# Attention in a hybrid backbone block: the weighted values of two query tiles in one product, with the values stationary

## The chip, the cores and the metric

The kernel runs on one core of a Trainium2 chip. A core has TensorE (PE in the profile, with its weight loads as PEld), VectorE (DVE), ScalarE (ACT), GpSimd (POOL), and SyncE (SP), which issues most DMA transfers. The metric is the device time of one launch in microseconds. The times known beforehand are 1080.52, 1079.1 and 1081.81 us: median 1080.52.

## The reference

The block has two layers over 1024 latent tokens of width 1024 and 256 context tokens. The even layer is a Fourier mixer and a differential attention side by side; the odd layer is a gated short convolution. The change concerns the attention alone:

```python
def one_block(qblk):
    s = jnp.einsum('bqhmd,bkhmd->bhmqk', qblk, k,
                   preferred_element_type=jnp.float32) * ATTN_SCALE
    p = jax.nn.softmax(s, axis=-1)
    a = p[:, :, 0] - lam * p[:, :, 1]
    return jnp.einsum('bhqk,bkhv->bqhv', a.astype(v.dtype), v)
...
ao = (rms_norm(attn_o, subln_g) * (1.0 - lam_init)).reshape(b, n, ATT_WIDTH)
y = jnp.concatenate([fo, ao], axis=-1) * jax.nn.silu(proj[..., G0:])
return y @ w_out
```

There are 4 heads. Each has two score maps (m = 0, 1) of 64 features, 1280 keys (256 of the context, 1024 latent), 1024 queries and values of 128 features. The second softmax is subtracted from the first with a learned factor; the weighted values are normalised by their RMS over the 128 features, scaled by a gain per feature, multiplied by a gate, and projected.

## The kernel before

A query tile is 128 queries of one head: 32 tiles, `i` = 0 to 31, eight to a head. Four tiles make a group `g` (half of a head's queries): eight groups. Keys come in ten blocks of 128 (`NK`). The keys and queries of the scores are float32 values split in two and stored in the rounded type fp32r (the profile prints them as f32 too); the weights `p`, their transposes `aT` and the values `v` are plain float32. The profile shows each plain float32 product as two passes, that is two weight loads and two matmuls.

In the attention loop the order of the work on TensorE, VectorE, ScalarE and GpSimd is written out by hand: an engine runs its instructions in the order in which the functions below are called (`manual_schedule(engines=MANUAL)`, L957). For a tile `i`:

- `score(i, m)` (L1025, L1026): twelve fp32r products in all for m = 0 and 1, into the PSUM tile S0 or S1. There is one S tile for each m, so the score of tile i+1 waits until `expo(i, m)` has read it.
- `rowmax(i, m)` (L1030): VectorE takes the negated row maximum over the 1280 keys. `expo(i, m)` (L1041): ScalarE takes the exponential and, by its accumulator, the row sum z.
- `combine(i)` (L1048 to L1055), called in the next tile: p0 minus lambda times z0/z1 times p1. VectorE does the first 1024 keys, GpSimd the last 256. The division by z0 is left to the RMS step, which cancels it but for the epsilon.
- `turn(i, c)` (L1065, L1067): TensorE transposes up to four key blocks of p0 into one PSUM bank (`ps_t`), ScalarE copies them to `aT`. Three turns of 4, 4 and 2 blocks make a tile.
- `values(i)` (L1075, L1084): ten products with the transposed weights stationary and 128 columns of `v` moving, into `ps_av` (queries on partitions); VectorE copies the result to a quarter of `o`.
- `squares(i)` (L1090): ScalarE squares that quarter and sums each row.
- `fin_a(g)` (L1096 to L1101) on GpSimd: the RMS factor from the sums and z0, its power -0.5, and the product with `o`.
- `fin_b(g)` (L1109 to L1115): four transposes of `o` into `ps_o`, product with gain and gate on VectorE, and the split into `yh` and `yl` for the output projection.

`turn`, `values` and `squares` lag the score by two or three tiles. `ps_t`, `ps_av` and `ps_o` all take turns in the two PSUM banks of the pool `pst` under the tag "t"; a new tile waits for the readers of the one that had its bank. The loads of the next head's keys, queries and values go through SP, 13 per head, three per tile from a head's third tile on. Behind the loop (L1186 on) the last tiles' turns and values are woven into the first two products of the output projection (`proj_feat2`, L1128 to L1130); the first of them needs groups 0, 2, 4 and 6 for its last four steps.

The broadcast of a row factor over the partitions by a diagonal (`rms_diag`, `ps_rows`, L228) and sums over partitions by a product with a column of ones (`token_sums`, L209) are used elsewhere in the kernel.

Of the kernel before, what the change touches and what calls it, by code (L numbers as in the profile page):

```python
# [33 lines left out]
S_C, S_G, S_B, S_CW, S_SUB, S_QG, S_KG, S_L = 0, 16, 32, 80, 104, 105, 169, 233  # L34
# [3 lines left out]
def block_kernel(tc, A):  # L38
    nc = tc.nc
# [34 lines left out]
    small = const.tile([P, S_N], F32, name="small")  # L74
# [3 lines left out]
    sel, ident = cst[:, 0:2], cst[:, 2:2 + P]  # L78
# [83 lines left out]
    wq, W, wsrc = [], [], []  # L162
# [857 lines left out]
    def score(i, m):  # L1020
        ks, qs, _ = preps[i // 8]
        q = qs[m][:, (i % 8) * P:(i % 8 + 1) * P]
        for c0, cn in CH:
            kc = slice(c0, c0 + cn)
            nc.tensor.matmul(S[m][:, kc], lhsT=q, rhs=ks[m][0][:, kc], start=True, stop=False)  # L1025
            nc.tensor.matmul(S[m][:, kc], lhsT=q, rhs=ks[m][1][:, kc], start=False, stop=True)  # L1026

    def rowmax(i, m):
        nm = av.tile([P, 1], F32, name=f"nm{m}", bufs=2)
        nc.vector.tensor_reduce(out=nm, in_=S[m][:, :NKEY], op=ALU.max, axis=AX.X, negate=True)  # L1030
        tiles[i, m, "nm"] = nm

    def expo(i, m):
        p = (pp, av)[m].tile([P, NKEY], F32, name=f"p{m}", bufs=(4, 2)[m])
        if m == 0:
            if i % 4 == 0:
                z0s[i // 4] = av.tile([P, 4], F32, name="z0", bufs=3)
            z = z0s[i // 4][:, i % 4:i % 4 + 1]
        else:
            z = av.tile([P, 1], F32, name="z1", bufs=2)  # L1040
        nc.scalar.activation(out=p, in_=S[m][:, :NKEY], func=AF.Exp, bias=tiles.pop((i, m, "nm")), accum_out=z)  # L1041
        tiles[i, m] = (p, z)
# [12 lines left out]
        nc.vector.scalar_tensor_tensor(out=p0[:, ks], in0=p1[:, ks], scalar=c, in1=p0[:, ks], op0=ALU.mult,  # L1055
                                       op1=ALU.add)

    def turn(i, c):

        n = min(4, NK - 4 * c)  # L1060
        pt = pst.tile([P, NB], F32, name="ps_t", tag="t", bufs=2)
        p0 = tiles[i, 0][0]
        for j in range(n):
            k = 4 * c + j
            nc.tensor.transpose(pt[:, j * P:(j + 1) * P], p0[:, k * P:(k + 1) * P], ident)  # L1065
        at = av.tile([P, NB], F32, name="aT", bufs=4)
        nc.scalar.copy(out=at[:, :n * P], in_=pt[:, :n * P])  # L1067
        groups[i, c] = at

    def values(i):  # L1070
        g, j = divmod(i, 4)
        v = preps[i // 8][2]
        ps = pst.tile([P, NB], F32, name="ps_av", tag="t", bufs=2)[:, :P]
        for k in range(NK):
            nc.tensor.matmul(ps, lhsT=groups[i, k // 4][:, (k % 4) * P:(k % 4 + 1) * P],  # L1075
                             rhs=v[:, k * P:(k + 1) * P], start=k == 0, stop=k == NK - 1)
# [7 lines left out]
        nc.vector.tensor_copy(out=o[:, j, :], in_=ps)  # L1084

    def squares(i):
        g, j = divmod(i, 4)
        o, ss, _ = groups[g, "f"]
        sq = av.tile([P, P], F32, name="osq", bufs=1)
        nc.scalar.activation(out=sq, in_=o[:, j, :], func=AF.Square, accum_out=ss[:, j:j + 1])  # L1090

    def fin_a(g, eng=nc.gpsimd):

        o, ss, _ = groups[g, "f"]
        z0 = z0s.pop(g)
        nc.gpsimd.tensor_tensor(out=z0, in0=z0, in1=z0, op=ALU.mult)  # L1096
        nc.gpsimd.tensor_scalar(out=z0, in0=z0, scalar1=EPS, scalar2=None, op0=ALU.mult)
        nc.gpsimd.tensor_scalar(out=ss, in0=ss, scalar1=1.0 / DV, scalar2=None, op0=ALU.mult)
        nc.gpsimd.tensor_tensor(out=ss, in0=ss, in1=z0, op=ALU.add)
        nc.gpsimd.tensor_tensor(out=ss, in0=ss, in1=mhalf[:, 0:4], op=ALU.pow)  # L1100
        eng.tensor_tensor(out=o, in0=o, in1=ss.unsqueeze(2).broadcast_to([P, 4, P]), op=ALU.mult)  # L1101

    def fin_b(g):

        f, half = NH + g // 2, g % 2
        o, _, sg = groups.pop((g, "f"))
        pt = pst.tile([P, NB], F32, name="ps_o", tag="t", bufs=2)
        for j in range(4):
            nc.tensor.transpose(pt[:, j * P:(j + 1) * P], o[:, j, :], ident)  # L1109
        y = av.tile([P, NB], F32, name="y", bufs=1)  # L1110
        nc.vector.scalar_tensor_tensor(out=y, in0=pt, scalar=g08, in1=sg, op0=ALU.mult, op1=ALU.mult)
        yh = yao.tile([P, NB], F32R, name="yh", tag="y", bufs=16)
        nc.scalar.copy(out=yh, in_=y)
# [43 lines left out]
    for i in range(NQ):  # L1157
        if i % 8 == 0 and i // 8 + 1 < NH:
            loads = att_prep(i // 8 + 1, nc.sync)
        if i % 8 > 1:  # L1160
            for _ in range(min(3, len(loads))):
                loads.pop(0)()
        score(i, 0)
        if i >= 2:
            turn(i - 2, 0)
            turn(i - 2, 1)
        rowmax(i, 0)
        if i:
            combine(i - 1)
        if i >= 3:  # L1170
            squares(i - 3)
        if i >= 6 and i % 4 == 2:
            fin_a((i - 6) // 4)
# [6 lines left out]
        if i >= 2:  # L1180
            values(i - 2)
        if i >= 7 and i % 4 == 3:
            fin_b((i - 7) // 4)
# [14 lines left out]
    pend = [proj_feat2(W[0], 0, {1: lambda: turn(NQ - 2, 2), 2: lambda: values(NQ - 2), 4: lambda: turn(NQ - 1, 0),
                                 5: lambda: (turn(NQ - 1, 1), squares(NQ - 2)), 7: lambda: turn(NQ - 1, 2)})]
    values(NQ - 1)  # L1200
    squares(NQ - 1)
# [560 lines left out]
```

## Time and profile before

| | before |
|---|---|
| median of three runs | 1080.52 us |
| the profiled execution, its span | 1081.25 us, 1079.4 us |
| TensorE, weight loads | 1031.8 us (96%), 843.3 us |
| VectorE, ScalarE, GpSimd | 760.0, 480.7, 436.8 us |
| value products (L1075), 640 passes | 76.8 us of modelled length |
| transposes of the weights (L1065), in the loop's 29 tiles | 290, 41.2 us of modelled length |
| first score of tile 2 to first score of tile 31 | 378.68 to 551.54 us |

The span is shorter than the time of the execution by what lies before the first and behind the last instruction. Busy shares are averages over stages with different limits. Lengths of matmuls overlap one another in the records, so what a matmul costs in a full stream is read from the distance between starts. A group's row gives the line, engine, operation, tiles, shapes and count, then the busy time, the mean length in ns, and the idle time ahead of it with what ended it.

### The profile page before, as it was taken

Reading aid. Unit: us, or ns where it says so; the run is one execution under the profiler, and the core shown is the slowest. Engines: PE = TensorE matmul, PEld = TensorE weight load, DVE = VectorE, ACT = ScalarE, POOL = GpSimd, SP = SyncE. Lnnn points to the kernel's source line nnn. Section 1 sums busy time; section 2 is a strip of 40 time slices with the busy share of each in tenths; the row PEclk is TensorE's granted clock in tenths of the full one; section 3 lists DMA queues with packets and bytes.
Section 4 is the critical chain, followed back from the end, with each engine's and each line's share of the span. In section 5 each row is a group of like instructions: output and inputs, shape, how many; then the busy total and the mean of one; then the engine's idle time right before and its main releaser. Section 6 shows DMA issues by size and latency. Waiting matters only on the chain.

```text
span 1079.4 us, 14123 instructions
## 1 busy us (share of the span) xinstructions
PE 1031.8 (96%) x5128; PEld 843.3 (78%) x5128; DVE 760.0 (70%) x1112; ACT 480.7 (45%) x876; POOL 436.8 (40%) x379
## 2 busy tenths in 40 slices
PE   6989999989999899999999999999999999998898
PEld 3667888878887699899988878777888888786676
DVE  4599956957888288888873386996555554579953
ACT  4453234312445377777763363634333333343420
POOL 1257115530454047775666644034443543402031
PEclk9999999999999999999999999999999999998999
DMA  9823896354111987081004643021112111113421
GB/s 335 339 97 117 253 370 225 108 152 136 43 61 66 249 196 177 25 190 52 18 21 156 198 156 134 0 78 60 59 39 75 43 60 59 59 39 107 145 99 58
DMA packets 61380, 131.12 MB, mean 121 GB/s; under 512 B 5248, under 2 KB 30208, under 8 KB 58112
## 3 DMA queue, kind: packets, MB, share of 16 engines
q1 hardware_dynamic: 60240, 125.64, 36.7%
q0 software_dynamic: 1072, 4.59, 1.2%
q8 instruction: 40, 0.66, 0.3%
q14 instruction: 28, 0.23, 0.1%
HBM read 105.57 MB, written 24.64 MB: 121 GB/s over the span
## 4 chain that ended last, share of the span: by engine, by line
PE 64%; DVE 21%; POOL 4%; ACT 4%; issue 3%; DMA 3%; SPq 0%; ACTq 0%; POOLq 0%; DVEq 0%
PE psX L657 6%; PE psX L659 6%; PE psX L658 6%; PE ps_av L1075 5%; PE ps_tok L284 3%; PE ps_tok L285 3%; PE ps_tok L286 3%; PE psY L658 3%; PE psY L659 3%; PE psY L657 3%; PE S L1025 3%; PE S L1026 3%; DVE nm L1030 2%; PE ps_t L1065 2%; DMA ada_raw<-in_ada_dram 2%
## 5 line engine op out<-in xcount | busy, mean ns | idle before, releaser
L284 PE MATMUL ps_tok<-whi,hhi 128*128 128x512 f32 x288 | 118.0, 410 | 2.5 <-ACT hhi L393 1.5
L285 PE MATMUL ps_tok<-whi,hlo 128*128 128x512 f32 x288 | 115.0, 399 | 3.5 <-DVE hlo L397 3.5
L286 PE MATMUL ps_tok<-wlo,hhi 128*128 128x512 f32 x288 | 114.8, 399 | 0.6 <-DVE wlo L172 0.4
L634 POOL TENSOR_TENSOR s<-wraw 128x512 f32<-128x512 f32 x20 | 26.7, 1333 | 212.5 <-DMA wraw<-in_wodd_dram 101.7
L1030 DVE TENSOR_REDUCE nm<-S 128x1 f32<-128x1280 f32 x64 | 95.2, 1487 | 22.0 <-PE S L1026 17.2
L1041 ACT ACTIVATE p<-S,nm 128x1280 f32<-128x1280 f32 x64 | 85.1, 1330 | 44.7 <-DVE nm L1030 40.9
L61 ACT CAST wop<-wraw 128x512 fp32r<-128x512 f32 x106 | 65.2, 619 | 82.7 <-PE ps_feat L1130 22.0
L657 PE MATMUL psX<-B,wop 128*128 128x512 f32 x240 | 95.6, 398 | 5.0 <-ACT u L1366 2.5
L659 PE MATMUL psX<-B,wop 128*128 128x512 f32 x240 | 95.3, 397 | 4.3 <-DVE wop L1312 4.3
L658 PE MATMUL psX<-B,wop 128*128 128x512 f32 x240 | 94.8, 395 | 0.0
L62 POOL TENSOR_TENSOR wop<-wraw,wop 128x512 fp32r<-128x512 f32 x52 | 71.5, 1377 | 42.1 <-ACT wop L61 42.0
L1075 PE MATMUL ps_av<-v,aT 128*128 128x128 f32 x640 | 76.8, 276 | 0.0
L1075 PEld LDWEIGHTS ps_av<-v,aT 128*128 128x128 f32 x640 | 74.2, 192 | 0.2
L285 PEld LDWEIGHTS ps_tok<-whi,hlo 128*128 128x128 f32 x288 | 55.1, 191 | 16.8 <-DVE hlo L397 6.0
L284 PEld LDWEIGHTS ps_tok<-whi,hhi 128*128 128x128 f32 x288 | 55.3, 192 | 16.2 <-issue 2.2
L1052 POOL TENSOR_TENSOR p<-p,cc 128x256 f32<-128x256 f32 x32 | 40.3, 1259 | 64.7 <-DVE cc L1049 45.1
L286 PEld LDWEIGHTS ps_tok<-wlo,hhi 128*128 128x128 f32 x288 | 55.1, 191 | 13.1 <-DVE wlo L172 1.4
L658 PE MATMUL psY<-B,wop 128*128 128x512 f32 x160 | 63.6, 397 | 1.7 <-DVE B L1259 1.7
L659 PE MATMUL psY<-B,wop 128*128 128x512 f32 x160 | 63.5, 397 | 0.0
L657 PE MATMUL psY<-B,wop 128*128 128x512 f32 x160 | 63.5, 397 | 0.0
L657 PEld LDWEIGHTS psX<-B,wop 128*128 128x128 f32 x240 | 45.1, 188 | 18.3 <-ACT u L1366 3.4
L659 PEld LDWEIGHTS psX<-B,wop 128*128 128x128 f32 x240 | 45.0, 188 | 17.0 <-DVE wop L1312 6.2
(354 smaller groups left out, 2694.5 us busy)
## 6 DMA issues: line engine op xcount, KB each, us to landing
ada_raw<-in_ada_dram SPq DMA_DIRECT2D x24, 1024.0 KB, 7.6
wraw<-in_wodd_dram SPq DMA_DIRECT2D x32, 512.0 KB, 3.5
wraw<-in_wo_dram SPq DMA_DIRECT2D x24, 512.0 KB, 4.1
wraw<-in_wtok_dram SPq DMA_DIRECT2D x16, 512.0 KB, 5.3
arena<-kd SPq DMA_DIRECT2D x16, 320.0 KB, 9.0
kq<-kd SPq DMA_DIRECT2D x16, 320.0 KB, 10.2
xt<-in_xT_dram SPq DMA_DIRECT2D x16, 256.0 KB, 6.3
xr<-in_xT_dram SPq DMA_DIRECT2D x16, 256.0 KB, 4.0
```

Of the source, the lines that this page charges most:

```text
L61: nc.scalar.copy(out=o[:, 0, :], in_=src)
L62: eng.tensor_tensor(out=o[:, 1, :], in0=src, in1=f32(o[:, 0, :]), op=ALU.subtract)
L284: nc.tensor.matmul(ps, lhsT=hh, rhs=whi, start=k == 0, stop=False)
L285: nc.tensor.matmul(ps, lhsT=hl, rhs=whi, start=False, stop=False)
L286: nc.tensor.matmul(ps, lhsT=hh, rhs=wlo, start=False, stop=k == KT - 1)
L657: nc.tensor.matmul(ps, lhsT=a, rhs=x[k][0], start=start and k == 0, stop=False, skip_group_check=not start)
L658: nc.tensor.matmul(ps, lhsT=a, rhs=x[k][1], start=False, stop=False, skip_group_check=not start)
L659: nc.tensor.matmul(ps, lhsT=b, rhs=x[k][0], start=False, stop=k == 3, skip_group_check=not start)
L1030: nc.vector.tensor_reduce(out=nm, in_=S[m][:, :NKEY], op=ALU.max, axis=AX.X, negate=True)
L1041: nc.scalar.activation(out=p, in_=S[m][:, :NKEY], func=AF.Exp, bias=tiles.pop((i, m, "nm")), accum_out=z)
L1052: nc.gpsimd.tensor_tensor(out=p1[:, ks], in0=p1[:, ks], in1=c.broadcast_to([P, POOLK]), op=ALU.mult)
L1075: nc.tensor.matmul(ps, lhsT=groups[i, k // 4][:, (k % 4) * P:(k % 4 + 1) * P], rhs=v[:, k * P:(k + 1) * P], start=k == 0, stop=k == NK - 1)
```

## The change

Query tiles are handled in pairs (`a` even, tiles a and a+1). A turn now transposes two key blocks of both tiles into one bank, so there are five turns of four transposes per pair, all copied as 128x512. `values` takes a block of `v` as the stationary operand and 256 columns of `aT` as the moving one, so `ps_av` comes out with the value features on partitions and the queries of two tiles along the row. `outputs` scales by the gain (per partition) on VectorE and squares on ScalarE, both straight from PSUM. The sum of squares over the features is now a sum over partitions: `fin_m` does four products with the squares stationary and one column of ones moving. `fin_d` adds the epsilon term, takes the power, and builds four diagonals on GpSimd; `fin_r` multiplies an all-ones matrix with them, which spreads the factor over the partitions; `fin_b` multiplies and splits as before. No output transposes are left. The gate is multiplied into `o` by `fin_a`. The factor 1/128 of the mean moves into the gain and the epsilon.

In an odd tile i (a = i-3) the loop does turns 0 to 3 of a pair and one of `fin_m` and `fin_r`; in the next, even tile it does turn 4 and all twenty passes of the pair's values, eight ahead of score(i,1) and twelve behind it. `outputs` follows in the next odd tile. `fin_b` stands ahead of `expo(i, 1)` on ScalarE. The new PSUM tile `ps_m` has the tag "t" too. `aT` has five buffers in place of four.

```diff
+    def turn(a, c):
         pt = pst.tile([P, NB], F32, name="ps_t", tag="t", bufs=2)
+        for n in range(4):
+            k, p0 = 2 * c + n // 2, tiles[a + n % 2, 0][0]
+            nc.tensor.transpose(pt[:, n * P:(n + 1) * P], p0[:, k * P:(k + 1) * P], ident)
+        at = av.tile([P, NB], F32, name="aT", bufs=5)
+        nc.scalar.copy(out=at, in_=pt)
+        groups[a, c] = at
+    def values(a, keys):
+        v = preps[a // 8][2]
+        if keys[0] == 0:
+            groups[a, "ps"] = pst.tile([P, NB], F32, name="ps_av", tag="t", bufs=2)[:, :2 * P]
+        for k in keys:
+            nc.tensor.matmul(groups[a, "ps"], lhsT=v[:, k * P:(k + 1) * P],
+                             rhs=groups[a, k // 2][:, (k % 2) * 2 * P:(k % 2 + 1) * 2 * P], start=k == 0,
+                             stop=k == NK - 1)
+    def outputs(a):
...
+        nc.vector.tensor_scalar(out=o[:, qs], in0=ps, scalar1=g08, scalar2=None, op0=ALU.mult)
+        nc.scalar.activation(out=sq[:, qs], in_=ps, func=AF.Square)
+    def fin_z(g):
+        z0 = z0s[g]
+        nc.gpsimd.tensor_tensor(out=z0, in0=z0, in1=z0, op=ALU.mult)
+        nc.gpsimd.tensor_scalar(out=z0, in0=z0, scalar1=EPS * DV, scalar2=None, op0=ALU.mult)
     def fin_a(g, eng=nc.gpsimd):
+        o, _, sg = groups[g, "f"]
+        eng.tensor_tensor(out=o, in0=o, in1=sg, op=ALU.mult)
+    def fin_m(g):
+        ps, sq, z0 = pst.tile([P, NB], F32, name="ps_m", tag="t", bufs=2)[:, :4], groups[g, "f"][1], z0s.pop(g)
+        for j in range(4):
+            nc.tensor.matmul(ps[:, j:j + 1], lhsT=sq[:, j * P:(j + 1) * P], rhs=ones[:, 0:1], start=True, stop=True)
+        groups[g, "m"] = ps, z0
+    def fin_d(g):
+        ps, z0 = groups.pop((g, "m"))
+        nc.vector.tensor_tensor(out=z0, in0=ps, in1=z0, op=ALU.add)
+        nc.gpsimd.tensor_tensor(out=z0, in0=z0, in1=mhalf[:, 0:4], op=ALU.pow)
+        dg = groups[g, "d"] = av.tile([P, 4, P], F32, name="dg", bufs=1)
+        nc.gpsimd.tensor_tensor(out=dg, in0=ident.unsqueeze(1).broadcast_to([P, 4, P]),
+                                in1=z0.unsqueeze(2).broadcast_to([P, 4, P]), op=ALU.mult)
+    def fin_r(g):
+        ps = groups[g, "r"] = pst.tile([P, NB], F32, name="ps_o", tag="t", bufs=2)
+        nc.tensor.matmul(ps, lhsT=ones, rhs=groups.pop((g, "d")).rearrange("p j d -> p (j d)"), start=True, stop=True)
     def fin_b(g):
+        y, _, _ = groups.pop((g, "f"))
+        nc.vector.tensor_tensor(out=y, in0=groups.pop((g, "r")), in1=y, op=ALU.mult)
         yh = yao.tile([P, NB], F32R, name="yh", tag="y", bufs=16)
         nc.scalar.copy(out=yh, in_=y)
...
+        odd, a = i % 2, i - 3 - (i + 1) % 2
         score(i, 0)
+        if a >= 2 and odd:
+            outputs(a - 2)
+        if a >= 0 and odd:
+            turn(a, 0)
+            turn(a, 1)
+        elif a >= 0:
+            turn(a, 4)
+            values(a, range(0, 4))
         rowmax(i, 0)
         if i:
             combine(i - 1)
+        if a >= 4 and a % 4 == 0 and odd:
+            fin_a((a - 4) // 4)
+        if a >= 2 and a % 4 == 2 and not odd:
+            fin_z((a - 2) // 4)
         expo(i, 0)
         score(i, 1)
+        if a >= 0 and odd:
+            turn(a, 2)
+            turn(a, 3)
+            if a >= 4 and a % 4 == 0:
+                fin_m((a - 4) // 4)
+            elif a >= 6:
+                fin_r((a - 6) // 4)
+        elif a >= 0:
+            values(a, range(4, NK))
         rowmax(i, 1)
+        if a >= 4 and a % 4 == 0 and odd:
+            fin_d((a - 4) // 4)
+        if a >= 6 and a % 4 == 2 and odd:
+            fin_b((a - 6) // 4)
         expo(i, 1)
...
+    turn(NQ - 4, 4)
+    values(NQ - 4, range(NK))
+    fin_r(NG - 2)
+    fin_b(NG - 2)
+    outputs(NQ - 4)
     combine(NQ - 1)
+    fin_z(NG - 1)
...
+    pend = [proj_feat2(W[0], 0, {2: lambda: turn(NQ - 2, 0), 3: lambda: turn(NQ - 2, 1),
+                                 4: lambda: turn(NQ - 2, 2), 5: lambda: turn(NQ - 2, 3),
+                                 6: lambda: turn(NQ - 2, 4)})]
+    values(NQ - 2, range(NK))
+    outputs(NQ - 2)
     fin_a(NG - 1, nc.vector)
+    pend.append(proj_feat2(W[1], 0, {2: lambda: (fin_m(NG - 1), fin_d(NG - 1)), 7: lambda: fin_r(NG - 1)}))
```

More of the change, by code (lines that the diff above doesn't have):

```diff
@@ L264, in lam @@
         nc.vector.tensor_scalar(out=neglam, in0=neglam, scalar1=-LAM0, scalar2=None, op0=ALU.add)
-        nc.vector.tensor_scalar(out=g08, in0=small[:, S_SUB:S_SUB + 1], scalar1=1.0 - LAM0, scalar2=None,
+        nc.vector.tensor_scalar(out=g08, in0=small[:, S_SUB:S_SUB + 1], scalar1=(1.0 - LAM0) * DV ** 0.5, scalar2=None,
                                 op0=ALU.mult)
@@ L1056, in combine @@
                                        op1=ALU.add)
-    def turn(i, c):
-        n = min(4, NK - 4 * c)
+    def turn(a, c):
         pt = pst.tile([P, NB], F32, name="ps_t", tag="t", bufs=2)
[L1062 to L1076, printed above, removed]
+        for n in range(4):
+            k, p0 = 2 * c + n // 2, tiles[a + n % 2, 0][0]
+            nc.tensor.transpose(pt[:, n * P:(n + 1) * P], p0[:, k * P:(k + 1) * P], ident)
@@ L1077, in values @@
+    def outputs(a):
+        g, j = divmod(a, 4)
         if j == 0:
-            o = av.tile([P, 4, P], F32, name="o", bufs=2)
-            ss = av.tile([P, 4], F32, name="ss", bufs=2)
+            o = av.tile([P, NB], F32, name="o", bufs=2)
+            sq = av.tile([P, NB], F32, name="osq", bufs=1)
             sg = av.tile([P, NB], F32, name="sga", bufs=2)
             nc.sync.dma_start(out=sg, in_=sgd[g // 2, :, (g % 2) * NB:(g % 2 + 1) * NB])
-            groups[g, "f"] = [o, ss, sg]
-        o, ss, _ = groups[g, "f"]
@@ L1084, in values @@
[L1084 to L1090, printed above, removed]
-    def fin_a(g, eng=nc.gpsimd):
[L1094 to L1101, printed above, removed]
+            groups[g, "f"] = [o, sq, sg]
@@ new lines, in outputs @@
+        o, sq, _ = groups[g, "f"]
+        ps, qs = groups.pop((a, "ps")), slice(j * P, (j + 2) * P)
+        nc.vector.tensor_scalar(out=o[:, qs], in0=ps, scalar1=g08, scalar2=None, op0=ALU.mult)
[4 more added lines that the diff above has]
+        nc.gpsimd.tensor_scalar(out=z0, in0=z0, scalar1=EPS * DV, scalar2=None, op0=ALU.mult)
+    def fin_a(g, eng=nc.gpsimd):
+        o, _, sg = groups[g, "f"]
+        eng.tensor_tensor(out=o, in0=o, in1=sg, op=ALU.mult)
@@ L1103, in fin_b @@
+    def fin_r(g):
+        ps = groups[g, "r"] = pst.tile([P, NB], F32, name="ps_o", tag="t", bufs=2)
+        nc.tensor.matmul(ps, lhsT=ones, rhs=groups.pop((g, "d")).rearrange("p j d -> p (j d)"), start=True, stop=True)
     def fin_b(g):
         f, half = NH + g // 2, g % 2
[L1106 to L1110, printed above, removed]
@@ L1169, in block_kernel @@
             combine(i - 1)
[L1170 to L1173, printed above, removed]
+        if a >= 4 and a % 4 == 0 and odd:
+            fin_a((a - 4) // 4)
+        if a >= 2 and a % 4 == 2 and not odd:
+            fin_z((a - 2) // 4)
         expo(i, 0)
         score(i, 1)
-        if i >= 2:
-            turn(i - 2, 2)
+        if a >= 0 and odd:
[7 more added lines that the diff above has]
+            values(a, range(4, NK))
         rowmax(i, 1)
+        if a >= 4 and a % 4 == 0 and odd:
+            fin_d((a - 4) // 4)
+        if a >= 6 and a % 4 == 2 and odd:
+            fin_b((a - 6) // 4)
         expo(i, 1)
[L1180 to L1183, printed above, removed]
         if i == 4:
@@ L1197, in block_kernel @@
     y0(0)
[L1198 to L1201, printed above, removed]
+    pend = [proj_feat2(W[0], 0, {2: lambda: turn(NQ - 2, 0), 3: lambda: turn(NQ - 2, 1),
[3 more added lines that the diff above has]
+    outputs(NQ - 2)
     fin_a(NG - 1, nc.vector)
-    pend.append(proj_feat2(W[1], 0))
+    pend.append(proj_feat2(W[1], 0, {2: lambda: (fin_m(NG - 1), fin_d(NG - 1)), 7: lambda: fin_r(NG - 1)}))
     w0next(eng=nc.vector)
```

9 lines of the change are left out of this document (removed).

## The prediction

> **What bounds the kernel now.** I read the page's busy times first, then the busy time by stage, for the stage in which the changed code runs: from the first score of query tile 2 to the first score of tile 31 (29 tiles), and from there to the end of the second projection.
>
> ```profile
> PE 1031.8 (96%) x5128; PEld 843.3 (78%) x5128; DVE 760.0 (70%) x1112; ACT 480.7 (45%) x876; POOL 436.8 (40%) x379
> ```
>
> ```profile
> core 0: us, PE busy (x) PEld busy (x) DVE busy (x) ACT busy (x) POOL busy (x), PEclk, DMA share, GB/s
> 378.68:551.54 172.86, 170.16 (x1242) 157.25 (x1243) 148.53 (x181) 129.89 (x269) 105.82 (x114) 1.00 0.42 102
> 551.54:577.40 25.86, 24.73 (x158) 21.24 (x157) 12.26 (x17) 11.84 (x27) 19.43 (x26) 1.00 0.06 21
> ```
>
> TensorE bounds the stage. VectorE comes next: 148.53/29 = 5.12 us a tile, against a tile of 172.86/29 = 5.96. Next the timeline of two tiles (start, length).
>
> ```profile
> 479.60 1.48 DVE L1030 TENSOR_REDUCE nm<-S 128x1 f32<-128x1280 f32 x1
> 481.17 1.33 ACT L1041 ACTIVATE p<-S,nm 128x1280 f32<-128x1280 f32 x1 [1.80 <-DVE nm L1030]
> 481.39 1.04 PE L1065 MATMUL ps_t<-cst,p 128*128 128x128 f32 x8
> 481.66 1.49 DVE L1030 TENSOR_REDUCE nm<-S 128x1 f32<-128x1280 f32 x1 [0.38 <-PE S L1026]
> 482.49 1.06 ACT L1067 COPY aT<-ps_t 128x512 f32<-128x512 f32 x2
> 482.64 0.50 PE L1025 MATMUL S<-arena 128*128 128x512 f32 x1 [0.21 <-ACT p L1041]
> 483.73 1.34 ACT L1041 ACTIVATE p<-S,nm 128x1280 f32<-128x1280 f32 x1
> 484.12 2.39 PE L1075 MATMUL ps_av<-v,aT 128*128 128x128 f32 x20
> 485.04 0.39 ACT L1067 COPY aT<-ps_t 128x256 f32<-128x256 f32 x1
> 486.36 0.60 PE L1109 MATMUL ps_o<-cst,o 128*128 128x128 f32 x4
> 486.71 0.48 PE L1025 MATMUL S<-arena 128*128 128x512 f32 x1
> 488.75 0.48 PE L1025 MATMUL S<-arena 128*128 128x512 f32 x1
> 492.36 0.48 PE L1025 MATMUL S<-arena 128*128 128x512 f32 x1
> ```
>
> Starts count, not the modelled lengths. Twenty value passes (two per f32 product, ten products) take 486.36-484.12 = 2.24 us, 0.112 each. Score and eight transposes take 488.75-486.71 = 2.04, score, two transposes and the values 492.36-488.75 = 3.61. So a transpose is 0.112, a score 1.15, and a tile without the final step 2 x 1.15 + 10 x 0.112 + 2.24 = 5.65 us of TensorE. Tile 19 (480.14 to 486.71) took 6.57: four output transposes (0.45) and waits for the exponential (482.64).
>
> TensorE's work in both stretches: 30 score tiles 68.8, 32 tiles of transposes and values 107.5, seven final steps 3.2, two projections of 24 products at 0.234 (neighbouring 512-column starts, below) 11.2: 190.7 of 198.7 us. So **8.0 us are waits**.
>
> **The change part by part.** (1) *Wide value products.* Twenty passes of 256 moving columns per pair replace forty of 128. Here is what f32 passes cost by width; the diagonal's row broadcast (L228) and the column sums (L209) exist elsewhere in this kernel.
>
> ```profile
> L1075 PE MATMUL ps_av<-v,aT 128*128 128x128 f32 x640 | 76.8, 276 | 0.0
> ```
>
> ```profile
> L228 PE MATMUL ps_r<-dg,ones x10: 379/592/1055, 17.0 to 668.0; 128*128 128x512 f32 x8, 128*128 128x256 f32 x2
> ```
>
> ```profile
> 662.34 0.28 PE L209 MATMUL ps_ss<-ones,x1ss 128*128 128x1 f32 x2
> ...
> 664.04 0.48 PE L657 MATMUL psZ<-arena,wop 128*128 128x512 f32 x1
> ...
> 667.62 1.02 PE L228 MATMUL ps_r<-dg,ones 128*128 128x512 f32 x2
> ...
> 668.70 0.39 PE L658 MATMUL psX<-arena,wop 128*128 128x512 f32 x1
> 668.93 0.39 PE L659 MATMUL psX<-arena,wop 128*128 128x512 f32 x1
> ```
>
> An f32 pass lasts 276 ns with 128 columns, 379 with 256 (the minimum) and 592 with 512 (the median): 213 ns for 256 columns more. From 667.62 to 668.70 lie two 512-column f32 passes and one product of the rounded type (fp32r, 668.93-668.70 = 0.23): (1.08-0.23)/2 = 0.425 a pass, 0.83 ns a column. A pass of 256 then spaces at 0.206 (from 379-276) to 0.224 (two narrow ones); I take 0.2145. Per pair 40 x 0.112 = 4.48 becomes 20 x 0.2145 = 4.29. **Gain 0.19 a pair, 3.0 us over 16 pairs** (0 to 5.8). Halving the number of weight loads buys next to nothing, since the columns streamed stay the same and the loads were hidden.
>
> By the back-to-back gap that the Trainium skill states in "TensorE: Matmul & The Clock Gate" (section Back-to-back issue gap), N/2.4 + 2.5 ns warm, a 256-column pass would space at 109 ns, and the values would cost 35 us in place of 72. The 379 ns row speaks against it for plain f32 operands. What it would make of the time is the third rival.
>
> (2) *Final step.* Four transposes (0.45) go. Four one-column products come, eight passes whose price is L209's, 1.70/16 to 0.112: 0.9; and a row broadcast, 2 x 0.425 = 0.85. That is +1.3 a group, **+10.4 over eight groups**. TensorE's work grows by 10.4-3.0 = 7.4 us.
>
> (3) *ScalarE, VectorE, GpSimd.*
>
> ```profile
> L1067 ACT COPY aT<-ps_t 128x512 f32<-128x512 f32 x58 | 31.0, 589 | 3.4 <-PE ps_t L1065 3.3
> L1055 DVE SCALAR_TENSOR_TENSOR p<-p,cc,p 128x1024 f32<-128x1024 f32 x30 | 43.1, 1436 | 1.1
> L1049 DVE SCALAR_TENSOR_TENSOR cc<-cc,neglam,z 128x1 f32<-128x1 f32 x29 | 8.8, 303 | 1.0
> L1048 DVE RECIPROCAL cc<-z 128x1 f32<-128x1 f32 x29 | 4.5, 154 | 0.0
> L1113 ACT CAST yh<-y 128x512 fp32r<-128x512 f32 x6 | 3.7, 615 | 0.0
> L1090 ACT ACTIVATE osq<-o 128x128 f32<-128x128 f32 x28 | 9.1, 326 | 0.0
> L1084 DVE COPY o<-ps_av 128x128 f32<-128x128 f32 x28 | 7.9, 283 | 3.7 <-PE ps_av L1075 3.7
> L1101 POOL TENSOR_TENSOR o<-o,ss 128x512 f32<-128x512 f32 x6 | 6.2, 1040 | 0.5
> L1111 DVE SCALAR_TENSOR_TENSOR y<-ps_o,g,sga 128x512 f32<-128x512 f32 x6 | 4.5, 748 | 0.6
> ```
>
> The square of 128x256 is not in the trace: 0.33 (128x128) to 0.59 (a 512 copy), I take 0.4; the VectorE output of 128x256 0.28 to 0.75, I take 0.42. ScalarE loses two squares and two short copies and gains one square and one full copy per pair: somewhat less work on an engine busy 130 of 173 us, which pays nothing. GpSimd's diagonal (1.04 by L1101) has two tiles, 12 us, before TensorE wants it. The gate rows' DMA on SP is issued with the pair's output and wanted two tiles later; a head's value tile is read until the third tile of the next head, before its reload, the last of 13 loads issued three per tile from that tile on. Nothing here. On VectorE fin_d waits for fin_m, to about 5.0 us behind score(i,0) on the count of the next part; the reduction ahead of it ends at 5.2, and behind it come the next tile's steps, so nobody waits for it in the loop.
>
> (4) *Two PSUM banks.* All of ps_t, ps_av, ps_m, ps_o take turns in two banks (tag t), so each waits until the one before the last is read. An odd tile now issues four turns and then the final step's product (fin_m or fin_r), which takes the bank of turn 2; turn 2's copy is queued on ScalarE **behind expo(i,0)**. Counting from the end of score(i,0) (481.39 above): reduction starts at 0.27 and ends at 1.76; the exponential starts 0.09 later (479.60+1.48 to 481.17) at 1.85; the next ScalarE instruction 1.31 later (483.73 to 485.04), at 3.16; its copy ends at 3.75; TensorE hears of it 0.14 later (481.17+1.33 to 482.64), 3.89. TensorE is there after four transposes twice over and a score: 0.90 + 1.15 + 0.90 = 2.95. **Wait 0.95 us**, in each of the 13 odd tiles 7 to 31: 12.4. Queued behind it are score(i+1,0), then the rest of TensorE. Before, the fourth bank of a tile only had to wait for a copy ahead of the exponential.
>
> (5) *Ends.* The lag of a pair leaves TensorE 2.3 us of work in tile 2 and 4.1 in tile 3, where VectorE needs 5.12: 2.8 + 1.0 = 3.8 lost. Behind the loop combine(31) stands on VectorE behind fin_b(6) and outputs(28), so behind fin_r(6). After fin_r: drain and handover 0.25, product 0.75, output 0.42, the two small ones 0.5, combine 1.44, handover 0.14 = 3.5; the projection offers two steps of 0.70 before it meets turn(30,0), which needs tile 31: 2.1 lost. The first value product there waits some 0.2 for fin_d.
>
> **Sum.** Work +7.4; waits 12.4 + 3.8 + 2.1 + 0.2 = 18.5 in place of 8.0: **+17.9 us**. The profiled execution took 1081.25 (span 1079.4), which is 0.7 above the median of 1080.52: 1081.25 + 17.9 = **1099 us**.
>
> **The rivals.** *No bank wait* (the wide turns' copies come early enough). The order on ScalarE speaks against it. Then another wait appears: in the six fin_r tiles 9 to 29 of the loop the cast of y stands ahead of expo(i,1). Reduction to 1.76, the small ones 0.5, combine 1.44, the second reduction 1.49: 5.2; product 0.75, cast 0.6, exponential 1.33, handovers 0.2: 8.1, where TensorE, with no bank wait, arrives at 2.95 + 0.85 + 1.15 + 0.45 + eight passes 1.7 = 7.1. Loss 1.0 x 6 = 6.0 (in the forecast the bank wait covers it). Total 7.4 + 6.0 + 3.8 + 2.1 + 0.2 - 8.0 = +11.5: 1093.
>
> *A slower clock as well.*
>
> ```profile
> 368.65:373.07 4.42, 2.72 (x13) 1.92 (x11) 2.27 (x3) 3.42 (x5) 0.00 (x0) 1.00 1.02 327
> 373.07:379.90 6.83, 6.23 (x15) 4.69 (x16) 5.55 (x6) 2.84 (x4) 2.15 (x2) 0.50 1.05 290
> ```
>
> After a stretch with TensorE 2.72 busy of 4.42, the clock stood at 0.50 for 6.83 us. Tiles 2 and 3 are now as thin (2.3 and 4.1 of 5.1); another such stretch over tile 4 costs up to 3.4 us, and a combine at its slow length (1.7) 0.2 in each fin_r tile: 1099 + 5 = 1104. The Trainium skill, same page, Part 1: The HAM clock gate, has a free-running window of about 3.4 us that sets the clock by how busy TensorE was; the 6.83 us row is two such windows.
>
> *The other side: a wide pass costs no more than a narrow one, 0.112.* Work then falls by 16 x 20 x 0.112 = 35.8, less 10.4. A pair would last: odd tile to the next score's end 3.89 + 0.87 + 1.15 = 5.9, even tile 0.45 + 20 x 0.112 + 2 x 1.15 = 5.0, so 10.9 against 2 x 5.96 = 11.9: -1.0 x 13, less 4.5 for the last two pairs' values, and back 7.4 at the ends (3.8 + 2.1 + 0.2 and 1.3 for the eighth group): -10.1, 1071. It holds while the square finds ScalarE free; where it waits for expo(i,1), TensorE's turn 1 waits with it and the gain is gone. The mechanism decides below about 0.17 us a pass; the 379 ns and 0.425 us rows stand against it.
>
> **How the numbers follow.** Forecast 0.60 (1095 to 1104 by its own bounds: 0 to 5.8 for the pass, 0.85 to 1.1 a bank wait); no bank wait 0.18; slower clock 0.13; cheap wide passes 0.06, most of it faster; 0.03 for something that hits neither. About 0.3% (3 us) is what a measurement of this kernel tells from no change. Faster 0.05, same 0.04, slower 0.91. The range runs from just under the second case to past the clock's case: 1089 to 1106.
>
> **What would show it.** Right: L1075 with 320 passes starting some 0.215 apart and lasting about 379 ns; TensorE waiting about 0.95 us for aT's copy before ps_m or ps_o in odd tiles; pairs of 12.9 us (odd 5.9, even 7.0); a wait of 2 us for combine before the first turn inside the projection. Wrong: passes 0.112 apart, or ps_m and ps_o starting at once behind the fourth turn.

## The result, and the profile after

The changed kernel takes 1096.91 us (median of three runs, 1092.18 to 1099.54) against 1080.52: a ratio of 1.0132, with a 95% interval of 1.0101 to 1.0164. It is slower, by 16.4 us; 1099 had been forecast. Its profiled execution took 1092.18 us, with a span of 1090.1.

First the busy times of the changed kernel's page, then its busy time by stage with the same marks as before: first score of tile 2 to first score of tile 31, to the end of the second projection product, to the last product. For the third stretch the row of the kernel before follows (columns as in the prediction; the number behind the stretch is its length).

```profile
PE 1030.2 (95%) x4856; PEld 836.1 (77%) x4856; DVE 754.9 (69%) x1103; ACT 479.0 (44%) x812; POOL 444.5 (41%) x371
```

```profile
375.44:561.05 185.61, 174.52 (x968) 150.31 (x969) 144.66 (x172) 127.97 (x210) 112.51 (x110) 0.99 0.38 97
561.05:593.90 32.85, 29.82 (x161) 25.05 (x160) 11.35 (x17) 12.42 (x23) 20.45 (x21) 1.00 0.09 33
593.90:1085.99 492.09, 476.80 (x2055) 384.31 (x2053) 322.21 (x478) 194.55 (x333) 175.98 (x127) 0.99 0.26 88
```

```profile
577.40:1075.05 497.65, 482.23 (x2057) 383.33 (x2055) 323.39 (x479) 194.91 (x333) 176.41 (x126) 0.99 0.26 88
```

The loop's 29 tiles went from 172.86 to 185.61 us, the end of the attention from 25.86 to 32.85: **19.7 us lost** where 17.9 were forecast. But the stretch behind it, whose code the change doesn't touch, is 5.6 us **shorter**. In this pair of profiles tile 2 also begins 3.2 us earlier; that start moves from run to run (378.4 and 377.4 us in another pair of the same two kernels). Together these make the 10.9 us between the two profiled executions. The changed kernel's was its fastest of three, 4.7 us below the median, so 5.5 of the 16.4 us lie in executions that were not profiled.

Next the value passes by tile, then the timeline of an odd tile of the changed kernel (start, length).

```profile
L1072 PE MATMUL ps_av<-aT,v x320: 377/379/472, 388.1 to 587.2; 128*128 128x256 f32 x160
L1087 DVE TENSOR_SCALAR o<-ps_av,g x16: 474/484/488, 393.8 to 587.7; 128x256 f32<-128x256 f32 x16
L1088 ACT ACTIVATE osq<-ps_av x16: 376/384/385, 394.3 to 588.2; 128x256 f32<-128x256 f32 x16
```

```profile
470.04 0.58 PE L1023 MATMUL S<-arena 128*128 128x512 f32 x1
...
471.66 1.49 DVE L1028 TENSOR_REDUCE nm<-S 128x1 f32<-128x1280 f32 x1 [0.75 <-PE S L1024]
...
473.19 1.33 ACT L1039 ACTIVATE p<-S,nm 128x1280 f32<-128x1280 f32 x1
...
473.43 1.04 PE L1061 MATMUL ps_t<-cst,p 128*128 128x128 f32 x8
...
474.50 1.06 ACT L1063 COPY aT<-ps_t 128x512 f32<-128x512 f32 x2
...
475.22 1.10 PE L1119 MATMUL ps_o<-dg,ones 128*128 128x512 f32 x2 [0.76 <-ACT aT L1063]
...
475.76 0.80 PE L1023 MATMUL S<-arena 128*128 128x512 f32 x1
...
480.65 2.75 PE L1072 MATMUL ps_av<-aT,v 128*128 128x256 f32 x12
...
483.05 0.59 PE L1023 MATMUL S<-arena 128*128 128x512 f32 x1
```

Twelve value passes take 2.75 us from 480.65, with a last pass of 0.38: (2.75-0.38)/11 = 0.216 from start to start. In f32 a pass of 256 columns costs nearly twice one of 128 (0.112). The order on ScalarE is as worked out: exponential at 473.19, turn 2's copy 1.31 later, and the final step's product waits for that copy. The eight transposes would have ended at 473.43 + 8 x 0.112 = 474.33; ps_o begins at 475.22, **0.9 us late**. The pair 470.04 to 483.05 takes 13.0 us. Twice the 5.96 of before is 11.9.

Behind the loop, the first turn inside the projection (TensorE and VectorE):

```profile
574.18 0.27 PE L1061 MATMUL ps_t<-cst,p 128*128 128x128 f32 x1
...
574.44 2.32 DVE L1053 SCALAR_TENSOR_TENSOR p<-p,cc,p 128x1024 f32<-128x1024 f32 x1
...
576.82 0.55 PE L1061 MATMUL ps_t<-cst,p 128*128 128x128 f32 x3 [2.37 <-DVE p L1053]
```

Tile 30's block goes through; tile 31's waits for combine(31), 2.4 us by the bracket.

### The profile page after: what moved, and what is told of

Read it like the earlier page. It is cut to its first block, busy times and chain, and to the rows that moved or that the text cites. A ratio compares the mean times of both kernels' runs of the same rounds, so it can differ in the third digit from the quotient of the medians.

```text
span 1090.1 us, 13452 instructions
## 1 busy us (share of the span) xinstructions
PE 1030.2 (95%) x4856; PEld 836.1 (77%) x4856; DVE 754.9 (69%) x1103; ACT 479.0 (44%) x812; POOL 444.5 (41%) x371
## 4 chain that ended last, share of the span: by engine, by line
PE 65%; DVE 19%; ACT 6%; POOL 4%; issue 4%; DMA 2%; SPq 0%; ACTq 0%; POOLq 0%; DVEq 0%
PE psX L655 6%; PE ps_av L1072 6%; PE psX L657 6%; PE psX L656 6%; PE ps_tok L282 3%; PE ps_tok L283 3%; PE ps_tok L284 3%; PE psY L657 3%; PE psY L655 3%; PE psY L656 3%; PE S L1023 3%; PE S L1024 3%; ACT p L1039 2%; PE ps_feat L1143 2%; PE ps_feat L1142 2%
## 5 line engine op out<-in xcount | busy, mean ns | idle before, releaser
L655 PE MATMUL psX<-B,wop 128*128 128x512 f32 x240 | 95.5, 398 | 5.7 <-ACT u L1396 3.5
L657 PE MATMUL psX<-B,wop 128*128 128x512 f32 x240 | 95.2, 397 | 4.5 <-DVE wop L1342 4.4
L656 PE MATMUL psX<-B,wop 128*128 128x512 f32 x240 | 94.4, 393 | 0.0
L62 POOL TENSOR_TENSOR wop<-wraw,wop 128x512 fp32r<-128x512 f32 x52 | 75.4, 1453 | 35.0 <-ACT wop L61 35.0
L1050 POOL TENSOR_TENSOR p<-p,cc 128x256 f32<-128x256 f32 x32 | 48.5, 1514 | 82.1 <-PE S L1024 48.0
L1072 PE MATMUL ps_av<-aT,v 128*128 128x256 f32 x320 | 74.0, 379 | 0.0
L1072 PEld LDWEIGHTS ps_av<-aT,v 128*128 128x128 f32 x320 | 58.5, 190 | 6.9
L655 PE MATMUL psY<-B,wop 128*128 128x512 f32 x160 | 63.3, 395 | 0.0
L656 PE MATMUL psY<-B,wop 128*128 128x512 f32 x160 | 62.5, 391 | 0.6 <-DVE B L1289 0.6
L657 PE MATMUL psY<-B,wop 128*128 128x512 f32 x160 | 63.1, 394 | 0.0
L655 PEld LDWEIGHTS psX<-B,wop 128*128 128x128 f32 x240 | 45.4, 189 | 17.8 <-ACT u L1396 4.4
L657 PEld LDWEIGHTS psX<-B,wop 128*128 128x128 f32 x240 | 45.5, 190 | 16.9 <-DVE wop L1342 6.7
```

The lines of the kernel that those rows point to most:

```text
L62: eng.tensor_tensor(out=o[:, 1, :], in0=src, in1=f32(o[:, 0, :]), op=ALU.subtract)
L655: nc.tensor.matmul(ps, lhsT=a, rhs=x[k][0], start=start and k == 0, stop=False, skip_group_check=not start)
L656: nc.tensor.matmul(ps, lhsT=a, rhs=x[k][1], start=False, stop=False, skip_group_check=not start)
L657: nc.tensor.matmul(ps, lhsT=b, rhs=x[k][0], start=False, stop=k == 3, skip_group_check=not start)
L1050: nc.gpsimd.tensor_tensor(out=p1[:, ks], in0=p1[:, ks], in1=c.broadcast_to([P, POOLK]), op=ALU.mult)
L1072: nc.tensor.matmul(groups[a, "ps"], lhsT=v[:, k * P:(k + 1) * P], rhs=groups[a, k // 2][:, (k % 2) * 2 * P:(k % 2 + 1) * 2 * P], start=k == 0,
```

## The experiments

All ran beside the kernel before on the same chip; ratios are to it, with 95% intervals. Three sets ran on three chips, where the kernel before had medians of 1081.95, 1082.54 and 1082.77 us, so a difference between runs of two sets carries up to 0.8 us of that. "Attention stage" is the distance in the profile from the first score of tile 2 to the end of the second projection product (198.7 before, 218.5 changed).

**The same two kernels again, and the changed one with the constant put back.** The change also takes out a constant that nothing reads; the part of the diff shown above leaves these two lines out. The first two runs have no edit. The third:

```diff
+    ones_dv = const.tile([P, 1], F32, name="ones_dv")
+    nc.vector.memset(ones_dv, 1.0 / P)
```

> The kernel before, unchanged, profiled on the chip on which the others of this set run. In the two profiles shown so far, neighbouring fp32r products of 512 columns behind the attention stand 0.2332 us apart in the kernel before and 0.2292 in the changed one, and so the changed kernel won back 5.6 us there. Theory A (this belongs to the execution or the chip, not to the kernel): here before and changed have the same spacing, and the difference in time between them is that of the attention stage alone, 17 to 21 us. Theory B (it belongs to the kernel, through where its tiles lie): before 0.233 and changed 0.229 again, difference 10 to 16 us.

> The changed kernel, unchanged, on the same chip. From the first score of tile 2 to the end of the second projection product 218 us (measured once so far), against 198.5 in the kernel before; pairs of 13.0 us. Theory A of the spacing: as in the kernel before on this chip. Theory B: 0.229 against 0.233.

> The changed kernel with the removed four-byte constant (ones_dv) put back, so that every tile behind it in the left pools lies where it lay before. Theory A of the spacing: no difference from the changed kernel, 0 us within 3. Theory B, in the form that the shift of the tiles sets the spacing: 0.233 as in the kernel before, and 5 to 6 us slower than the changed kernel.

Measured: before 1083.72 (1.0016, 1.0005 to 1.0028, though it is the same kernel: 0.2% is not told apart here), changed 1096.00 (1.0134, 1.0117 to 1.0151), changed with the constant 1103.75 (1.0200, 1.0173 to 1.0228). A window of 100 us in the odd layer shows the spacing: passes counted behind the first figure. One line each of the kernel before, the changed one with the constant, and the changed one.

```profile
800.00:900.00 100.00, 100.00 (x430) 80.39 (x430) 57.91 (x92) 37.22 (x63) 42.98 (x32) 1.00 0.16 53
```

```profile
800.00:900.00 100.00, 100.00 (x431) 80.39 (x430) 53.69 (x88) 36.37 (x61) 41.26 (x30) 1.00 0.17 54
```

```profile
800.00:900.00 100.00, 100.00 (x438) 81.96 (x437) 53.79 (x82) 36.48 (x62) 44.98 (x33) 1.00 0.16 53
```

430, 431, 438: with the clock at 1.00 throughout, TensorE gets through 1.7% more products in the same time where the constant is missing. Neighbouring starts lie 0.2332, 0.2332 and 0.2292 us apart. So theory B holds: it belongs to the kernel. Nothing reads the constant, so it can act only through where the other tiles lie; the addresses themselves are in no run. The edit that only seems to tidy up **gave back 5.4 us behind the attention** (497.7 to 492.3, the profiles of these two runs). Between the medians of four executions each lie 7.8 us (1103.75-1096.00). That the other 2.4 belong to the constant is not shown: the profiled run with the constant has two stretches of 3.41 us at half the granted clock in the attention stage (from 547.08 and from 584.60) that the changed kernel's two profiles lack; where they lie 3.5 us were lost. Before the constant's removal is counted, the change costs 2.0%.

**The constant in the kernel before: taken away, and made wide.**

```diff
-    ones_dv = const.tile([P, 1], F32, name="ones_dv")
-    nc.vector.memset(ones_dv, 1.0 / P)
```

```diff
-    ones_dv = const.tile([P, 1], F32, name="ones_dv")
+    ones_dv = const.tile([P, 16], F32, name="ones_dv")
```

> The kernel before without the four-byte constant ones_dv, which nothing reads; no other edit. Theory (the constant moves every tile of the left pools by 32 bytes against those of the right pools, and that sets the fp32r spacing at 0.2332 or 0.2292): spacing 0.2292, 5.5 us less behind the second projection product, some 7 us less in all, 1075. Rival (the changed kernel's other tiles do it, or the stage behind it differs for its own reasons): no change, 0 within 2.

> The kernel before with ones_dv made 64 bytes wide in place of 4, so that the left pools move by 32 bytes the other way. Theory (what counts is where tiles lie modulo 64 bytes): as without the constant, spacing 0.2292 and some 7 us less. Rival (less room taken, or any other address, is what counts): no gain, 0.2332.

Measured: 1076.98 without it (0.9943, 0.9922 to 0.9965; 5.3 us of the gain behind the attention), 1070.39 with 64 bytes (0.9887, 0.9868 to 0.9906). The same window, without it and with 64 bytes:

```profile
800.00:900.00 100.00, 100.00 (x438) 81.91 (x438) 56.45 (x92) 38.45 (x65) 45.36 (x33) 1.00 0.16 53
```

```profile
800.00:900.00 100.00, 100.00 (x442) 82.79 (x442) 57.09 (x93) 37.61 (x63) 45.26 (x33) 1.00 0.16 53
```

Without the constant the spacing is 0.2292, as expected. With 64 bytes it is 0.2267 in this window and 0.2271 over the whole stretch behind the attention, better than either: the theory's form (only the place modulo 64 bytes counts) falls, and so does its rival, since more room was taken and the time fell. Three widths of the constant gave three spacings. They are not the same for all products: without the constant the three products of a step of the odd layer (L655, L656, L657) are followed by the next start after 0.232, 0.227 and 0.229 us on average, while the 512-column products of the scores keep 0.231 to 0.233 in all these runs. So it differs from one pair of operands to another. How the two have to lie is open. This kernel, equal to the one before but for the width of a constant that nothing reads, **beats both**.

**The final step's product one tile later.**

```diff
         elif a >= 0:
+            if a >= 4 and a % 4 == 0:
+                fin_m((a - 4) // 4)
+            elif a >= 6:
+                fin_r((a - 6) // 4)
             turn(a, 4)
             values(a, range(0, 4))
+            if a >= 4 and a % 4 == 0:
+                fin_d((a - 4) // 4)
+            elif a >= 6:
+                fin_b((a - 6) // 4)
...
             turn(a, 3)
-            if a >= 4 and a % 4 == 0:
-                fin_m((a - 4) // 4)
-            elif a >= 6:
-                fin_r((a - 6) // 4)
...
```

The calls of fin_d and fin_b behind rowmax(i, 1) go as well, and group 6's fin_m and fin_d move behind the loop.

> The final step's product (fin_m, fin_r) is called one tile later, ahead of turn 4 and behind score(i,0) of the even tile, with fin_d and fin_b behind it. Theory of the banks: when TensorE gets there, turn 2's copy has long been made (at 3.8 us behind the odd score, TensorE at 4.1), so the wait of 0.9 us before ps_m and ps_o goes; the values' bank then waits some 0.2 to 0.7 us for fin_d or fin_b. Attention stage 6 to 8 us shorter than the changed kernel. Rival (the ring of exponential, reduction and combine on ScalarE and VectorE sets the pair of 13 us, and the bank wait only uses time that would be waited elsewhere): less than 2 us shorter, the wait shows at the scores.

Measured: 1095.98 (1.0131, 1.0116 to 1.0146), no gain. The waits of TensorE's weight loads between 400 and 555 us, first of the changed kernel, then of this one (sum, times, longest):

```profile
PEld ps_m L1105 <- ACT aT L1063: 5.5, 6, 1.0
```

```profile
PEld S L1023 <- ACT p L1039: 4.5, 12, 0.5
PEld ps_av L1072 <- DVE o L1124: 2.9, 5, 0.6
...
PEld ps_t L1061 <- ACT osq L1088: 1.7, 5, 0.4
```

The bank wait is gone, and three others stand in its place: the score's for the exponential, the values' bank for fin_b, turn 1's for the square. The loop went from 185.79 to 184.52; in the end behind it this profile has a half-speed stretch of 3.41 us (582.70 to 586.11), which the changed kernel's profiles lack. The rival is right **for this edit**: the product went out of the odd tile, and the score's wait for the exponential is one of those that took the bank wait's place. It does not say what the bank wait alone is worth; the next one does.

**ps_m out of the ring of banks.**

```diff
-        ps, sq, z0 = pst.tile([P, NB], F32, name="ps_m", tag="t", bufs=2)[:, :4], groups[g, "f"][1], z0s.pop(g)
+        ps = S[1][:, NKEY:NKEY + 4] if g < NG - 1 else pst.tile([P, NB], F32, name="ps_m", tag="t", bufs=2)[:, :4]
+        sq, z0 = groups[g, "f"][1], z0s.pop(g)
```

> The changed kernel with the four columns of ps_m in the unused end of the second score tile (its third bank holds 256 columns of scores), in place of a bank of the ring, in seven of eight groups; the order of the work is the changed kernel's. Theory of the banks: the wait of 0.85 us before ps_m goes and nothing takes its place; 6 us less in the attention stage, in pairs with fin_r the wait stays. Rival (the ring of exponentials takes the wait over, as in the run with the final step one tile later): under 2 us.

Measured: 1090.62 (1.0079, 1.0059 to 1.0099), some 5.4 us under the changed kernel's 1096.00. Odd tiles with fin_m fall from 6.00 to 5.08 us, even ones stay at 6.99; the loop goes from 185.79 to 180.13, 5.7 us less. TensorE's waits, 400 to 555 us, of the changed kernel and of this one:

```profile
PE ps_o L1119 <- ACT aT L1063: 4.5, 6, 0.8
PE ps_m L1105 <- ACT aT L1063: 4.1, 6, 0.8
```

```profile
PE ps_o L1120 <- ACT aT L1063: 3.5, 6, 0.6
PE S L1023 <- ACT p L1039: 0.2, 1, 0.2
```

That of ps_m is gone and next to nothing follows. So the wait for turn 2's bank is a cost of its own, 0.9 us each. Behind the loop 3.7 us were lost again (36.5 in place of 32.8), for two reasons: the GpSimd power and diagonal of group 6 came to stand behind other GpSimd work, and TensorE stood idle 2.7 us for them ahead of fin_r; and the clock stood at half speed from 577.35 to 580.76.

**Narrow products.**

```diff
-        for k in keys:
-            nc.tensor.matmul(groups[a, "ps"], lhsT=v[:, k * P:(k + 1) * P],
-                             rhs=groups[a, k // 2][:, (k % 2) * 2 * P:(k % 2 + 1) * 2 * P], start=k == 0,
-                             stop=k == NK - 1)
+        for n, k in [(n, k) for n in range(2) for k in range(NK)][2 * keys[0]:2 * keys[-1] + 2]:
+            nc.tensor.matmul(groups[a, "ps"][:, n * P:(n + 1) * P], lhsT=v[:, k * P:(k + 1) * P],
+                             rhs=groups[a, k // 2][:, ((k % 2) * 2 + n) * P:((k % 2) * 2 + n + 1) * P],
+                             start=k == 0, stop=k == NK - 1)
```

> The changed kernel with each value product split in two of 128 columns, the values stationary as before the split: 640 passes in place of 320, all else as it is. Theory (an f32 pass is paid by its columns): passes 0.112 apart, 40 x 0.112 = 4.48 us a pair in place of 20 x 0.2145 = 4.29, so 3 us slower in all, 0 to 6. Rival (wide products save the weight loads): 20 or more us slower.

Measured: 1099.22 (1.0146, 1.0110 to 1.0181), 3.2 us over the changed kernel, whose interval overlaps. The profile is sharper: passes 0.112 apart, pairs of 13.14 in place of 13.00, the loop 1.9 us longer. **The wide product, the core of the change, is worth about 2 us.**

**No final product.** fin_m, fin_d and fin_r return at once, and fin_b multiplies by a constant, so the output is not normalised:

```diff
-        nc.vector.tensor_tensor(out=y, in0=groups.pop((g, "r")), in1=y, op=ALU.mult)
+        nc.vector.tensor_scalar(out=y, in0=y, scalar1=0.01, scalar2=None, op0=ALU.mult)
```

> The changed kernel without the final step's products: fin_m, fin_d and fin_r are left out, and fin_b multiplies by a constant, so the output is not normalised. It leaves out 8 x 1.75 = 14 us of TensorE's work and the bank wait of 12 us. Theory of the prediction's second case (behind the bank wait stands another: the cast of y ahead of the exponential): 13 to 16 us faster than the changed kernel, with a wait of about 1 us at the score behind each tile that calls fin_b. Simple theory (what TensorE is spared is won): 26 us faster, no new wait.

Measured: 1078.35 (0.9958, 0.9938 to 0.9978), 17.7 under the changed kernel; the attention stage is 16.6 shorter (202.0). That is a little over the chain's 13 to 16 and far from 26. The new wait is there, shorter than said (19 in the loop, the longest 0.7):

```profile
PEld S L1023 <- ACT p L1039: 9.9, 19, 0.7
```

**Rounded operands in the changed kernel.** aT, both value tiles and the tile in which the values are made become fp32r; head 0's values get a tile of that type in the old one's place. The main lines:

```diff
-        at = av.tile([P, NB], F32, name="aT", bufs=5)
+        at = av.tile([P, NB], F32R, name="aT", bufs=5)
...
-    heads = [(v0, arena), (at1.tile([P, NKEY], F32, name="v1"),
+    heads = [(at0.tile([P, NKEY], F32R, name="v2", tag="v0", bufs=1), arena), (at1.tile([P, NKEY], F32R, name="v1"),
```

> The changed kernel with the value products in the rounded type: aT and the values are fp32r tiles, so the weights and values are rounded and a product is one pass. By the 512-column fp32r products a pass of 256 columns costs 0.115 us, a pair's values 1.15 us in place of 4.29, 50 us less of TensorE's work over 16 pairs. Theory (two banks, ScalarE's order and VectorE's 5.1 us a tile bound the loop as soon as the passes are cheap): 11 to 18 us faster than the changed kernel, with waits of 1 to 2 us before turn 1 for the square behind expo, and the same wait before ps_m and ps_o. Rival (TensorE's passes are what counts): 40 or more us faster.

Measured: 1081.64 (0.9991, 0.9974 to 1.0007), 14 us under the changed kernel, where 11 to 18 was the theory of waits and 40 the rival. The weight loads' waits, 400 to 555 us:

```profile
PEld ps_t L1061 <- ACT osq L1088: 19.5, 12, 2.9
PEld S L1023 <- ACT p L1039: 10.3, 17, 0.9
...
PEld ps_m L1105 <- ACT aT L1063: 4.6, 6, 1.0
```

The values' passes fall by more than two thirds, and most of it comes back as waits, the largest before turn 1, for the square that stands behind the exponential. It is the wait that the prediction's third rival named as the one that would undo it.

**Combine first.**

```diff
     fin_r(NG - 2)
+    combine(NQ - 1)
     fin_b(NG - 2)
     outputs(NQ - 4)
-    combine(NQ - 1)
```

> Behind the loop, combine(31) is called ahead of fin_b(6) and outputs(28) on VectorE. Theory: the wait of about 2 us for combine before the first turn inside the projection goes; the end of the second projection product comes 1.3 to 2 us earlier, which is less than the spread of the times but shows in the profile. Rival (something else is late there, such as the values' bank): the wait stays, 0.

Measured: 1092.19 (1.0086, 1.0056 to 1.0116); the attention stage 215.5, 3.1 us shorter than the changed kernel's 218.6. The end behind the loop is 2.0 us shorter (30.9 for 32.8), the upper end of what was expected; the other 1.1 lie in the loop, which this edit doesn't touch (at its start the clock was another, see below). TensorE's waits from the last tile to the end of the second projection product, first of the changed kernel, then of this one:

```profile
PE ps_t L1061 <- DVE p L1053: 2.4, 1, 2.4
PE ps_m L1105 <- ACT aT L1063: 0.7, 1, 0.7
```

```profile
PE ps_m L1105 <- ACT aT L1063: 0.7, 1, 0.7
PE ps_o L1119 <- POOL dg L1113: 0.4, 1, 0.4
```

The wait for combine is gone, and one of 0.4 us for group 6's diagonals came in its place.

**Rounded operands in the kernel before**, without the constant: the same edits with the old orientation, 128 columns of `v` moving.

> The kernel before without ones_dv, and with the transposed weights and the values as fp32r tiles: both are rounded, and a value product is one pass. The products keep 128 moving columns. Theory (one pass costs the 0.112 that one of the two costs now; the loop is then set by VectorE's 5.1 us a tile and the ring of score, reduction and exponential): 10 us less in the attention stage than the kernel without ones_dv, in all 16 to 18 us below the kernel before, 1065. Rival (a narrow fp32r pass costs as much as two f32 passes): nothing beyond the gain of the layout, 1075.

Measured: 1066.06 (0.9849, 0.9827 to 0.9870). The attention stage takes 191.2 us against 199.6 without the rounding: 8.4 less, near the 10 expected. Eight such passes, and six of 256 columns in the changed kernel with rounding:

```profile
471.24 1.09 PE L1073 MATMUL ps_av<-v,aT 128*128 128x128 f32 x8
```

```profile
479.36 0.87 PE L1072 MATMUL ps_av<-aT,v 128*128 128x256 f32 x6
```

With a last pass of 0.28 (the median of either is 276 to 280 ns) the starts lie on average (1.09-0.28)/7 = 0.116 and (0.87-0.28)/5 = 0.118 apart. In the rounded type a pass of 256 columns costs what one of 128 does. There wide products would nearly halve the values' passes; in plain f32 they don't.

## Why the prediction was right or wrong

The direction and the size came out, 16.4 for 17.9. The mechanism did too, but that the two numbers lie so close is in part luck: all of the 17.9 had been placed in the attention stage, which lost 19.7, and 5.6 came back behind it, where the prediction had nothing.

*What bounds the kernel.* Right: the loop lost what TensorE was given to do and to wait for.

*Wide products.* Right in kind. A pass measured 0.216, not 0.2145, so 4.32 a pair against 4.47: 2.4 us in all, not 3.0.

*Final step.* Right. The product of the squares took 0.91 us (566.14 to 567.05 behind the loop), 0.9 forecast. The row broadcast took 0.85 as forecast: 0.54 to the next score's first start (475.22 to 475.76), and the second start came 0.31 later behind it than in other scores.

*Nothing on the other engines.* Right in the sum. The two unseen operations measured 484 ns (0.42 taken) and 384 ns (0.4).

*Two PSUM banks.* Right, and shown by taking ps_m out of the ring: 0.92 us a tile, where 0.95 was worked out. By the starts, ps_m and ps_o came 0.82 to 0.93 us late in each of the 13 tiles, 11.3 in all, not 12.4.

*Ends.* Tiles 2 to 5 took 22.6 us (375.44 to 398.02) for 17.5 us of TensorE's work by the prediction's prices, 5.1 lost where 3.8 was forecast. Here the clock has a part in it. The first row is a half-speed window of the changed kernel, the second are the same four tiles in the run with combine first, where the clock stood at full speed throughout.

```profile
378.38:381.79 3.41, 3.31 (x9) 2.73 (x10) 2.51 (x5) 1.47 (x3) 2.38 (x2) 0.50 1.03 246
```

```profile
378.94:400.59 21.65, 18.87 (x104) 15.84 (x104) 18.52 (x22) 15.15 (x25) 9.52 (x9) 1.00 0.95 231
```

There 4.1 were lost, near the forecast. The wait for combine(31) was 2.4 by the bracket instead of 2.1, with that combine at 2.32 us, not 1.44. The wait for fin_d is not there: the values followed turn 4 at 567.53 without one.

*Sum.* By the measured sizes the stage loses 10.5 (final step) - 2.4 (passes) + 11.3 (banks) + 5.1 + 2.4 (ends) - 8.0 (the waits of before) = 18.9 of the 19.7 us seen. The step that failed is the one left out: **the removal of the four-byte constant**. It is a line of the change, and no term was given to it, because it moves no work. It was worth -5.4 us behind the attention (-5.3 in the kernel before). With the constant in place the change costs 1103.75-1081.95 = 21.8 us, against 17.9 forecast. In that run's profile the stage takes 222.1 us for 198.7, and 3.5 of these 23.4 go with two half-speed windows, one in the loop at 547.08 and this one, in the projection just behind the wait for combine:

```profile
584.60:588.01 3.41, 3.41 (x13) 2.82 (x12) 0.00 (x0) 1.17 (x2) 0.26 (x2) 0.50 0.02 5
```

It cost 1.7 us there (34.5 in place of 32.8 from the loop's end to the end of the projection). The slower clock, the second rival, thus comes and goes with the run. Seven profiles of the changed kernel and its variants have the wait of 2.4 us for combine; in five of them a half-speed window begins 0.05 to 1.4 us behind it, and in the two of the changed kernel itself none does. The Trainium skill (TensorE: Matmul & The Clock Gate, Part 1: The HAM clock gate) speaks of a free-running window of about 3.4 us; the length of the 3.41 us rows agrees.

*The rivals.* No bank wait: not so, the wait was in all 13 tiles. The wait said to lie behind it, at the score for the exponential, exists (the run without final product), at most 0.7 us; that the cast of y alone makes it was not tried. Cheap wide passes: false for f32, and the run with rounded operands, where they are cheap, shows that this alone would have brought the changed kernel only to where the kernel before stands.

## What to carry to other kernels

Before making a product wider to save weight loads, look whether the loads are what is paid: if a wider pass of the same type is longer in proportion, nothing is saved, and what was rearranged for it (here a final step of 1.3 us more a group, a ring of two banks with one more tenant) is cost with next to no return. When a tile is put into a ring of banks, ask on which engine the reader of the tile two places before it is queued, and behind what. And give a term to every line of a diff that changes where tiles lie: time the kernel with that line alone.

## What the runs showed of the hardware that was not expected

- The spacing of 512-column fp32r products changes with the width of an unread constant that is allocated ahead of other tiles, at the same granted clock: over the stretch behind the attention 0.2332, 0.2293 and 0.2271 us with a four-byte constant, none, and a 64-byte one. On one chip the kernel took 1082.8, 1077.0 and 1070.4 us. The expectations put this down to where the tiles lie; no run shows the addresses or moved one operand alone, so the rule behind it is open.
- A single wait of TensorE of 2.4 us was followed by a window of 3.41 us at half the granted clock in five of seven profiles, at a cost of 1.7 us where it could be compared (34.5 for 32.8).
- An fp32r pass of 128 moving columns spaces at 0.116 us on average, one of 256 at 0.118, while f32 passes of these widths space at 0.112 and 0.216. Rounding, not width, is what shortens the values here.
